# Two attentions in a written order, rope by halves, PSUM pools kept: many small edits to a two-block fp32 kernel

## The chip, the cores and the metric

One core of one Trainium2 chip. The metric is the time on the device of one execution in microseconds, median over the runs. TensorE is called PE below, its weight loads PEld, VectorE DVE, ScalarE ACT, GpSimd POOL, and SyncE, which issues nearly all DMAs, SP.

## What is computed

Two blocks on a sequence of 512 tokens of width 1024, all in float32. Block one puts 16 meta tokens ahead (528 columns) and adds to h in turn a SwiGLU layer, a mixer of two attentions, and a second SwiGLU layer, each behind a norm and followed by one:

```python
h = h + 0.5 * rmsnorm(swiglu(rmsnorm(h, g1), wg, wu, wd), post1)
p = rmsnorm(h, g) @ w_in            # sb_q sb_k sb_v c_q c_kv k_r gates
y_sb  = stick_breaking_attention(sb_q, sb_k, sb_v) @ w_sb_o    # 8 heads
q = rmsnorm(c_q) @ w_uq             # 64 plain + 32 turned dims per head
y_mla = latent_attention(q_nope, rope(q_rope), k_nope, rope(k_r), v) @ w_mla_o
h = h + rmsnorm((sigmoid(g_sb) * y_sb + sigmoid(g_mla) * y_mla) @ w_out, post2)
h = h + 0.5 * rmsnorm(swiglu(rmsnorm(h, g3), ...), post3)
```

Rope turns each pair (x1, x2) of half vectors to (x1 cos - x2 sin, x1 sin + x2 cos). Block two has two layers: a recurrence with an mLSTM (called hy), then attention in a window (swa), each followed by a convolved feed-forward layer (convffn) and a gated addition (ple).

## The kernel before, in words

Activations lie transposed, features on partitions and tokens on columns. Each float32 product is three passes of a rounded type: `whi` and `wlo` are a weight tile's high and low parts (ACT casts, DVE subtracts the cast, in `wload`, L286 and L287), `xh` and `xl` those of the activations. A linear with 8 k-tiles and 512 columns is 24 matmuls of 128x512 (L301 in `mm`, L328 in `lin_first`, which starts a phase with several outputs together). Raw weights (`wraw`) come by DMA in SP's order.

PSUM has pools named by `psums`: l (linears) and a (everything small) in most phases, z, l and a with two banks each in the two attentions. Each phase opens its own pools, and `rstd` sums the squares over partitions by a product with ones (L393), after DVE has added the eight squared tiles into `acc` (L247).

The scheduler orders all engines but, in the attentions, PE follows a hand-written order: for each pair of heads c and block b of 128 queries, `start` issues the scores (L721) and masks (L724), `chain` the softmax on ACT and DVE, `attn_t` transposes the probabilities `e` (L672, L684), and `attn_v` multiplies by the values (L695). Between them `fill(n)` puts n steps of the linears in `todo` (L343, `step_lin`): the next pair's projections, the gates, the output products. `step_lin` with `two=True` fills two banks (256 and 272 columns) in turns for `sbk` and the latent keys. In `attn_t` and `attn_v` all instructions stand in a block of raised priority, those of PE too.

In `latent`, two of the four pairs share a rope product: `uq` tiles 4 to 7 are the rope columns and the same columns with halves swapped, `t12` holds the two products with cos and sin, and DVE adds them into rows 64 to 95 of each q (96 rows). ACT copies q, k and the common `kr` rows into new tiles for each pair. `values` (L910) is computed between the first projection and the first scores. All 16 gate sigmoids stand before `latent`. In `hy`, `heads` ends with four transposes of `nm` back (L1120), directly behind the norm's scaling on DVE (L1119).

Of the kernel before, what the change touches and what calls it, by code (L numbers as in the profile page):

```python
# [72 lines left out]
def prep(inp):  # L73
# [18 lines left out]
    r["uq"] = np.concatenate([_wt(nope), _wt(rope), _wt(_swap(rope, 16))], axis=0)  # L92
# [72 lines left out]
def consts():  # L165
# [23 lines left out]
    r["rope"] = np.ascontiguousarray(rope.astype(np.float32))  # L189
# [26 lines left out]
class Kern:  # L216
    def __init__(self, tc, d, voff):
        self.tc, self.nc, self.d, self.voff = tc, tc.nc, d, voff
        self.act_cur, self.act_pre, self.act_epoch = None, None, []

# [33 lines left out]
    def psums(self, st, **bufs):  # L254
        self.psp = {n: st.enter_context(self.tc.tile_pool(name="ps" + n, bufs=b, space=PSUM, reuse_waits="tile"))
                    for n, b in bufs.items()}
# [23 lines left out]
    def wload(self, src, n, ahead=100):  # L280
        nc = self.nc
        raw = self.early.pop(0) if self.early else self.wdma(src, n)
        hi = self.wp.tile([P, 1024], F32R, name="whi", bufs=WB[1])[:, :n]
        lo = self.wp.tile([P, 1024], F32R, name="wlo", bufs=WB[1])[:, :n]
        with self.tc.high_priority(offset=ahead):
            nc.scalar.copy(hi, raw)  # L286
            nc.vector.tensor_tensor(lo, raw, hi, op=ALU.subtract)  # L287
# [48 lines left out]
    def step_lin(self, src, x, kc, done, c0=0, two=False):  # L336

        hi, lo = self.wload(src, kc * P, 2000)
        segs, ev = self.banks2() if two else self.banks1(c0)
        for k in range(kc):  # L340
            for pi, (a, b) in enumerate(((hi, x[0]), (hi, x[1]), (lo, x[0]))):
                for ps, t0, t1 in segs:
                    self.nc.tensor.matmul(ps, a[:, k * P:(k + 1) * P], b[:, k, t0:t1],  # L343
                                          start=k == 0 and pi == 0, stop=k == kc - 1 and pi == 2)
                yield
        with self.tc.high_priority(offset=1000):
            done(ev)
# [38 lines left out]
    def rstd(self, acc, tt, tb, dim, pool_r, name="r"):  # L386
# [5 lines left out]
        for i, (c, w) in enumerate(blocks):  # L392
            nc.tensor.matmul(ps[:w, i * 64:(i + 1) * 64], acc[:, c:c + w], self.ones[:, :64], start=True, stop=True)  # L393
# [52 lines left out]
    def square(self, acc, m, parts):  # L446
# [4 lines left out]
        for p, a, b in parts:  # L451
            self.act(sq[:, a:b], p, AF.Square)
        if m:
# [18 lines left out]
    def begin(self, st):  # L472
# [14 lines left out]
        nc.sync.dma_start(self.vecs, d["vecs"])  # L487
# [3 lines left out]
    def begin2(self):  # L491
        self.nc.sync.dma_start(self.cst, self.d["cst"])
# [3 lines left out]
    def ffn(self, n, h, tt, name):  # L496
# [5 lines left out]
        self.psums(n.st, l=6, a=2)  # L502
# [51 lines left out]
    def mixer(self, n, h):  # L554
        nc, d, tc = self.nc, self.d, self.tc
        mul, add = ALU.mult, ALU.add
        stP = ExitStack()
        self.psums(stP, l=6, a=2)
# [11 lines left out]
        with ExitStack() as stS:  # L570
# [3 lines left out]
            with ExitStack() as st:  # L574
                A = self.pool(st, "mA")
                rope = A.tile([64, 2, TM], F32, name="rope64")
                nc.sync.dma_start(rope, d["rope"][:64])
# [47 lines left out]
            stP.close()  # L625
            stP = ExitStack()
# [881 lines left out]
```

## Time and profile before

| what | value |
|---|---|
| median of 3 runs | 2532.71 us (2532.6 to 2533.84) |
| the profiled execution | 2533.2 us |
| its span, first to last instruction | 2531.4 us |
| PE busy | 2496.9 us (99%) |
| DVE, ACT, POOL busy | 54%, 39%, 6% |
| granted PE clock, mean | 1.0 |

The profile is of one core. A matmul's record runs from its start to a modelled end, and the next one may start before that. "Idle <- releaser" is the time in which the engine had no instruction, and what it waited for.

### The profile page before, as it was taken

The numbers are of one execution on the slowest core, as the hardware profiler recorded it, in microseconds if no ns is written. First come the engines' busy times: TensorE is split into PE (matmuls) and PEld (weight loads), VectorE is DVE, ScalarE is ACT, GpSimd is POOL, SyncE is SP. The second block draws the span as 40 slices with busy tenths as digits, with TensorE's granted clock in tenths as the row PEclk, the third lists the DMA queues.
The fourth block names the chain that finished last, engine by engine and source line by source line (L and its number), as shares of the span: only waits on it lengthen the run. The fifth ranks groups of instructions, "written<-read, shape, count | busy, mean of one in ns | idle before, by whom it ended". The sixth has DMA issues, their size and how long they took to land.

```text
span 2531.4 us, 33257 instructions
## 1 busy us (share of the span) xinstructions
PE 2496.9 (99%) x13334; PEld 2081.7 (82%) x13334; DVE 1360.7 (54%) x2197; ACT 993.6 (39%) x1601; POOL 162.3 (6%) x159
## 2 busy tenths in 40 slices
PE   8999999999999999999999999999999999999999
PEld 8999998777677788888777888888888668888887
DVE  5323347455566562434668765345465775535544
ACT  4222235344654442223564633223344563323332
POOL 1101010000001010101001011001000001101100
PEclk9999999999999999999999999999999999999999
DMA  4322234212212433333322332332333123333332
GB/s 140 92 92 85 92 95 132 81 54 67 59 43 64 161 116 92 97 100 98 115 89 90 118 107 91 93 109 92 93 114 101 42 76 133 94 98 100 96 89 100
DMA packets 78932, 240.49 MB, mean 95 GB/s; under 512 B 9332, under 2 KB 11636, under 8 KB 78520
## 3 DMA queue, kind: packets, MB, share of 16 engines
q1 hardware_dynamic: 78776, 238.35, 30.4%
q8 instruction: 105, 1.72, 0.3%
q14 instruction: 51, 0.42, 0.1%
HBM read 226.24 MB, written 8.92 MB: 93 GB/s over the span
## 4 chain that ended last, share of the span: by engine, by line
PE 91%; DVE 4%; ACT 3%; issue 1%; DMA 1%; POOL 0%; SPq 0%; ACTq 0%; DVEq 0%
PE l L301 71%; PE l L328 5%; PE l L343 5%; PE l L314 2%; PE z L721 1%; PE a L695 1%; PE a L672 1%; ACT e L236 1%; PE s L1414 1%; DVE wlo L287 1%; ACT whi L286 1%; PE a L408 1%; PE a L393 1%; DMA wraw<-in_hyo 1%; PE a L1442 1%
## 5 line engine op out<-in xcount | busy, mean ns | idle before, releaser
L286 ACT CAST whi<-wraw 128x1024 fp32r<-128x1024 f32 (+4 forms) x456 | 432.9, 950 | 1032.1 <-PE l L301 781.7
L301 PE MATMUL l<-xh,whi 128*128 128x512 f32 (+3 forms) x2156 | 707.9, 355 | 0.0
L301 PE MATMUL l<-xh,wlo 128*128 128x512 f32 (+3 forms) x2156 | 705.8, 354 | 0.0
L301 PE MATMUL l<-xl,whi 128*128 128x512 f32 (+3 forms) x2156 | 705.5, 354 | 0.0
L287 DVE TENSOR_TENSOR wlo<-wraw,whi 128x1024 fp32r<-128x1024 f32 (+4 forms) x456 | 500.2, 1098 | 274.9 <-ACT whi L286 268.8
L301 PEld LDWEIGHTS l<-xh,whi 128*128 128x128 f32 (+1 forms) x2156 | 382.1, 188 | 56.9 <-issue 1.4
L301 PEld LDWEIGHTS l<-xh,wlo 128*128 128x128 f32 (+1 forms) x2156 | 381.9, 188 | 56.6 <-issue 1.0
L301 PEld LDWEIGHTS l<-xl,whi 128*128 128x128 f32 (+1 forms) x2156 | 382.2, 187 | 56.2 <-issue 1.2
L301 PE MATMUL l<-chh,wlo 128*128 128x512 f32 x384 | 149.4, 389 | 0.0
L301 PE MATMUL l<-chl,whi 128*128 128x512 f32 x384 | 149.4, 389 | 0.0
L301 PE MATMUL l<-chh,whi 128*128 128x512 f32 x384 | 149.4, 389 | 0.0
L301 PE MATMUL l<-hh,wlo 128*128 128x256 f32 (+2 forms) x528 | 140.3, 320 | 0.0
L301 PE MATMUL l<-hl,whi 128*128 128x256 f32 (+2 forms) x528 | 140.2, 320 | 0.0
L301 PE MATMUL l<-hh,whi 128*128 128x256 f32 (+2 forms) x528 | 140.1, 319 | 0.0
L247 POOL TENSOR_TENSOR t<-g,xrs 128x528 f32<-128x528 f32 (+1 forms) x44 | 75.1, 1708 | 646.0 <-ACT g L236 646.0
L247 POOL TENSOR_TENSOR cc<-cc,xrs 128x512 f32<-128x512 f32 x48 | 62.8, 1308 | 834.1 <-ACT cc L236 830.3
L247 DVE TENSOR_TENSOR t<-l,t 128x256 f32<-128x256 f32 (+1 forms) x66 | 32.3, 516 | 143.9 <-PE l L301 138.9
L301 PEld LDWEIGHTS l<-hh,whi 128*128 128x128 f32 x528 | 88.4, 188 | 6.9
L301 PEld LDWEIGHTS l<-hl,whi 128*128 128x128 f32 x528 | 88.2, 188 | 6.9
L301 PEld LDWEIGHTS l<-hh,wlo 128*128 128x128 f32 x528 | 88.3, 188 | 6.8
L247 DVE TENSOR_TENSOR g<-l,xrs 128x256 f32<-128x256 f32 (+1 forms) x66 | 32.3, 516 | 114.3 <-PE l L301 112.6
L247 DVE TENSOR_TENSOR cz<-l,xrs 128x512 f32<-128x512 f32 x48 | 33.2, 692 | 109.6 <-PE l L301 105.3
(350 smaller groups left out, 3463.6 us busy)
## 6 DMA issues: line engine op xcount, KB each, us to landing
wraw<-in_up SPq DMA_DIRECT2D x96, 512.0 KB, 3.5
wraw<-in_dn SPq DMA_DIRECT2D x64, 384.0 KB, 3.2
wraw<-in_ffn_g SPq DMA_DIRECT2D x44, 512.0 KB, 3.5
wraw<-in_ffn_u SPq DMA_DIRECT2D x44, 512.0 KB, 3.4
wraw<-in_ffn_d SPq DMA_DIRECT2D x32, 448.0 KB, 3.3
wraw<-in_hy SPq DMA_DIRECT2D x20, 512.0 KB, 3.5
wraw<-in_ffn_d SPq DMA_DIRECT2D x16, 512.0 KB, 3.6
wraw<-in_gate SPq DMA_DIRECT2D x16, 512.0 KB, 3.5
```

What stands on the lines that cost most here:

```text
L236: i = nc.scalar.activation(out, in_, f, **kw)
L247: return (eng or self.nc.vector).tensor_tensor(out, a, b, op=op)
L286: nc.scalar.copy(hi, raw)
L287: nc.vector.tensor_tensor(lo, raw, hi, op=ALU.subtract)
L301: self.nc.tensor.matmul(ps, a[:, k * m:(k + 1) * m], b[:, k0 + k, c0:c1], start=first and k == 0 and pi == 0, stop=last and k == kc - 1 an ...
L314: self.nc.tensor.matmul(ps[:c1 - c0, :n], a[:, k, c0:c1], b[:, j * n:(j + 1) * n], start=k == 0 and pi == 0, stop=k == nk - 1 and pi == 2)
L328: self.nc.tensor.matmul(ps, a[:, k * P:(k + 1) * P], b[:, k0 + k, t0:t1], start=k == 0 and pi == 0, stop=k == kc - 1 and pi == 2)
L343: self.nc.tensor.matmul(ps, a[:, k * P:(k + 1) * P], b[:, k, t0:t1], start=k == 0 and pi == 0, stop=k == kc - 1 and pi == 2)
L393: nc.tensor.matmul(ps[:w, i * 64:(i + 1) * 64], acc[:, c:c + w], self.ones[:, :64], start=True, stop=True)
L408: nc.tensor.matmul(p[:, c - a:c - a + w], r[:w, i:i + 1].to_broadcast([w, P]), self.ident[:w, :w], start=True, stop=True)
L672: nc.tensor.transpose(pt[:, j * P:(j + 1) * P], probs[hh][:, i * P:(i + 1) * P], self.ident)
L695: nc.tensor.matmul(po[64 * hh:64 * hh + 64, :], vt[:, i, (2 * c + hh) * 64:(2 * c + hh + 1) * 64], where[(i, hh)], start=i == 0, stop=i == nb)
```

## The change

1. **Begin.** The first 8 columns of `vecs` and the first tile of h are loaded ahead of all weights; the first two weight tiles are loaded and cast in pieces of 256 and 768 columns.
2. **PSUM.** `psums` keeps the pools if the next phase asks for the same; the last phase of swa asks for l=6, a=2 like its neighbours.
3. **`step_lin` with two=True** computes the first half (256 columns) over all k, hands it on, then the second.
4. **Attentions.** In `attn_t` and `attn_v` only the copies keep the raised priority; PE's instructions stand in the order in which they are written.
5. **Latent.** The rope columns of all 8 heads are ordered by halves (two tiles, 18 matmuls in place of 36); six DVE instructions give `turned` once, DMAs of 32 rows put it into q (now 128 rows), k are four standing tiles whose `kr` rows are put there by DMA. The first projection's copies go to DVE, `values` behind the first scores; each pair has two `wo` products to fill with (before 2, 1, 2, 3). Only `gs` sigmoids stand ahead; those of `gm` go into the `wo` loop.
6. **w_out** splits its first weights at priority 2000.
7. **Squares.** The last of the eight squares isn't added by DVE: PE sums it in `rstd` with a second set of small matmuls, in the same bank (after ffn1, mixer and ffn2).
8. **hy.** The transposes back become `back`, called behind a further linear.

The core of the diff:

```diff
+    def psums(self, **bufs):
+        if bufs == self.ps_bufs:
+            return
+        self.ps_st.close()
...
-    def lin_first(self, srcs, x, kc, c0=0, wide=False, two=False, k0=0):
-        ws = [self.wload(src, kc * P) for src in srcs]
+    def lin_first(self, srcs, x, kc, c0=0, wide=False, two=False, k0=0, ahead=100):
+        ws = [self.wload(src, kc * P, ahead) for src in srcs]
...
     def step_lin(self, src, x, kc, done, c0=0, two=False):
-        segs, ev = self.banks2() if two else self.banks1(c0)
-        for k in range(kc):
+        for c0, c1 in ((0, CUT), (CUT, TM)) if two else ((c0, c0 + T),):
+            ps = self.bank()[:, :c1 - c0]
+            for k in range(kc):
...
+            with self.tc.high_priority(offset=1000):
+                done(ps, c0, c1)
...
+        accs = acc if isinstance(acc, list) else [acc]
+        for j, a in enumerate(accs):
+            for i, (c, w) in enumerate(blocks):
+                nc.tensor.matmul(ps[:w, i * 64:(i + 1) * 64], a[:, c:c + w], self.ones[:, :64],
...
+        if m == KD - 1:
+            return [acc, sq]
...
-        with self.tc.high_priority(offset=100):
-            for g0 in range(0, len(slots), 4):
+        for g0 in range(0, len(slots), 4):
...
+            with self.tc.high_priority(offset=100):
                 (nc.vector.tensor_copy if (g0 // 4) % 2 else nc.scalar.copy)(at[:, :n1], pt[:, :n1])
...
+                for s_ in range(2):
+                    p = 64 + 32 * s_ + 16 * hh
+                    nc.sync.dma_start(k[p:p + 16, :], kr[16 * s_:16 * s_ + 16, :])
...
+                        self.tt(turned[:, j, :], ps, rope[:, 0, :], mul)
+                        self.tt(t[:, 1 - j, :], ps, rope[:, 1, :], mul)
+                        if j:
+                            self.tt(turned[:, 0, :], turned[:, 0, :], t[:, 0, :], ALU.subtract)
+                            self.tt(turned[:, 1, :], turned[:, 1, :], t[:, 1, :], add)
...
-            nm = (2, 1, 2, 3)[c]
+            nm = 2
...
-            self.fill(6)
+            if c == 0:
+                values()
+            else:
+                self.fill(4)
...
-        first = self.lin_first([d["wout"][m] for m in range(2)], oo, KD)
+        first = self.lin_first([d["wout"][m] for m in range(2)], oo, KD, ahead=2000)
...
-            heads(hd, segs[hd])
+            nm = heads(hd, segs[hd])
+            if hd < 2:
+                z_of(5 + 2 * hd, bias=False, out=gg[:, 2 * hd + 1, :])
...
+            back(hd, nm)
-        kn.early.append(kn.wdma(d[("ffn1_g", "ffn1_u")[k]][0], D))
+        for a, b in ((0, 2 * P), (2 * P, D)):
+            for w, nm in zip(kn.early, ("ffn1_g", "ffn1_u")):
+                dma(w[:, a:b], d[nm][0][:, a:b])
```

Three places where the order of instructions moves. **PE, stick-breaking attention, first pair of heads, block 0 to 1.** z are scores, a<-cst,e the transposes of the probabilities, idb the mask's product, l<-x a linear step. Before:

```order
L343 MATMUL l_5010<-xl_4215,whi_5006 128x512
L721 MATMUL z_5051<-sbk_4911,sbq_4910 128x272 x2
L672 MATMUL a_5103<-cst_62,e_5024 128x128 x2
L684 MATMUL a_5103<-cst_62,e_5024 16x128 x2
L724 LDWEIGHTS idb_65
L724 MATMUL z_5051<-masks_4362,idb_65 128x128
```

Now:

```order
L354 MATMUL l_5085<-xl_4227,whi_5081 128x256
L690 MATMUL a_5106<-cst_62,e_5028 128x128 x2
L703 MATMUL a_5106<-cst_62,e_5028 16x128 x2
L354 MATMUL l_5085<-xh_4226,wlo_5082 128x256
L354 MATMUL l_5085<-xh_4226,whi_5081 128x256
```

The transposes stood right behind block 1's scores and ahead of their masks; now the masks come first and 24 linear matmuls stand between the scores and the transposes.

**PE, the same stage, the keys' projection `sbk`.** l_5081 and l_5082 are its two banks before, l_5085 and l_5119 now. Before:

```order
L343 MATMUL l_5081<-xh_4214,whi_5077 128x256
L343 MATMUL l_5082<-xh_4214,whi_5077 128x272
L343 MATMUL l_5081<-xl_4215,whi_5077 128x256
L343 MATMUL l_5082<-xl_4215,whi_5077 128x272
L343 MATMUL l_5081<-xh_4214,wlo_5078 128x256
L343 MATMUL l_5082<-xh_4214,wlo_5078 128x272
```

Now:

```order
L354 MATMUL l_5085<-xl_4227,whi_5081 128x256
L354 MATMUL l_5085<-xh_4226,wlo_5082 128x256
L354 MATMUL l_5119<-xh_4226,whi_5081 128x272
L354 MATMUL l_5119<-xl_4227,whi_5081 128x272
L354 MATMUL l_5119<-xh_4226,wlo_5082 128x272
```

Both banks ended together; now the first is complete 24 matmuls before the second.

**SP, from the stick-breaking to the latent attention.** wraw are weight tiles, rope the tables. Before:

```order
L277 DMA wraw_6635<-in_uk 128x256 [waits DMAHW3_49,DVE_49]
L830 DMA rope_6570<-in_rope 128x1056 [waits DVE_49,PE_49,Pool_49]
L277 DMA wraw_6663<-in_uv 128x1024 [waits DMAHW4_49,DVE_49]
L277 DMA wraw_6724<-in_uq 128x384 [waits DMAHW5_49,DVE_49]
L277 DMA wraw_6760<-in_uk 128x256 [waits DMAHW7_49,DVE_49]
```

Now (behind rope8 and seven DMAs of kr):

```order
L863 DMA k11_6568<-kr_4362 16x528 [waits DMAHW1_49,Pool_49]
L890 DMA q0_6637<-turned_6581 32x512 [waits DMAHW2_49,DVE_49]
L890 DMA q0_6637<-turned_6581 32x512 [waits DMAHW3_49]
L890 DMA q1_6641<-turned_6581 32x512 [waits DMAHW4_49]
L890 DMA q1_6641<-turned_6581 32x512 [waits DMAHW5_49]
L890 DMA q0_6804<-turned_6581 32x512 [waits DMAHW6_49]
L890 DMA q0_6804<-turned_6581 32x512 [waits DMAHW7_49]
L890 DMA q1_6808<-turned_6581 32x512 [waits DMAHW0_49]
L890 DMA q1_6808<-turned_6581 32x512 [waits DMAHW1_49]
L863 DMA k11_6568<-kr_4362 16x528 [waits DMAHW2_49]
L285 DMA wraw_6753<-in_uq 128x384 [waits DMAHW3_49,Activation_49]
L285 DMA wraw_6812<-in_uk 128x256 [waits DMAHW4_49,DVE_49]
```

The weights of the second pair stood behind the tables alone; now they stand behind eight DMAs that wait for `turned`.

## Rows read from the trace of the kernel before

**Rows 1.** The page's part 1, busy time of each engine over the span.

```profile
PE 2496.9 (99%) x13334; PEld 2081.7 (82%) x13334; DVE 1360.7 (54%) x2197; ACT 993.6 (39%) x1601; POOL 162.3 (6%) x159
```

**Rows 2.** Stages: window, length, busy PE, PEld, DVE, ACT, POOL, granted clock, DMA share, GB/s.

```profile
684.00:694.00 10.00, 7.63 (x39) 6.25 (x38) 6.62 (x10) 9.83 (x19) 0.00 (x0) 1.00 0.42 115
694.00:795.00 101.00, 98.63 (x657) 72.58 (x656) 63.78 (x178) 54.90 (x145) 0.00 (x0) 1.00 0.14 43
```

**Rows 3.** Timeline of the beginning: start us, us, engine, line, operation, [idle before <-releaser].

```profile
1.65 0.43 SPq L1463 DMA_DIRECT2D h<-in_xT  x1
...
7.32 0.73 ACT L244 ACTIVATE xh<-h,vecs 128x528 fp32r<-128x528 f32 x1 [1.56 <-DMA h<-in_xT]
...
8.11 0.58 PE L328 MATMUL l<-xh,whi 128*128 128x256 f32 x1 [8.11 <-ACT xh L244]
```

**Rows 4.** DMA issues over the span: KB each, us from issue to landing.

```profile
qt<-ra SPq DMA_DIRECT2D x32, 64.0 KB, 2.0
...
rope<-in_rope SPq DMA_DIRECT2D x1, 528.0 KB, 3.7
...
vecs<-in_vecs SPq DMA_DIRECT2D x1, 213.5 KB, 2.6
```

**Rows 5.** Timeline of PE where hy and its feed-forward layer begin.

```profile
1233.31 0.47 PE L301 MATMUL l<-pph,whi 128*128 128x512 f32 x1 [0.88 <-ACT whi L286]
...
1461.74 0.47 PE L328 MATMUL l<-xh,whi 128*128 128x512 f32 x1 [1.63 <-DVE h L247]
```

**Rows 6.** Groups of instructions on PE, whole span: busy, mean ns | idle before <-releaser.

```profile
L343 PE MATMUL l<-xh,whi 128*128 128x512 f32 (+2 forms) x224 | 79.2, 370 | 2.1 <-DVE sbk L247 2.1
L672 PE MATMUL a<-cst,e 128*128 128x128 f32 x160 | 27.1, 282 | 5.1 <-ACT e L236 3.9 <-DVE e L894 1.1
```

**Rows 7.** Timeline of PE at a rope product of the latent stage.

```profile
683.12 0.39 PE L343 MATMUL l<-cqh,whi 128*128 128x512 f32 x1
683.35 0.39 PE L343 MATMUL l<-cql,whi 128*128 128x512 f32 x1
```

**Rows 8.** Timeline from the last stick-breaking product to the end of the latent stage.

```profile
678.02 0.44 PE L695 MATMUL a<-rest,sbv 128*64 128x128 f32 x4
678.54 0.33 SPq L830 DMA_DIRECT2D rope<-in_rope  x1
684.65 0.69 DVE L247 TENSOR_TENSOR t<-l,rope 128x512 f32<-128x512 f32 x1
691.13 0.40 PE L343 MATMUL l<-ckvh,whi 128*128 128x272 f32 x1 [2.37 <-ACT q L243]
...
736.63 0.39 PE L343 MATMUL l<-ckvh,whi 128*128 128x272 f32 x1 [0.73 <-ACT q L243]
...
791.13 0.44 PE L672 MATMUL a<-cst,e 128*128 128x128 f32 x2 [1.09 <-DVE e L894]
```

**Rows 9.** Stages, the columns of rows 2: the first matmuls of the program.

```profile
8.10:13.40 5.30, 5.28 (x19) 4.47 (x20) 4.12 (x6) 4.93 (x8) 0.00 (x0) 1.00 1.01 385
```

**Rows 10.** Timeline at the first products of w_out.

```profile
816.54 1.22 DVE L287 TENSOR_TENSOR wlo<-wraw,whi 128x1024 fp32r<-128x1024 f32 x1
...
817.82 0.50 PE L328 MATMUL l<-ooh,wlo 128*128 128x512 f32 x1 [1.50 <-DVE wlo L287]
```

**Rows 11.** Timeline of PE at the sums of squares after ffn1 and the mixer.

```profile
404.41 1.12 PE L393 MATMUL a<-cst,acc 128*88 128x64 f32 x12 [0.81 <-DVE acc L247]
...
864.48 1.08 PE L393 MATMUL a<-cst,acc 128*128 128x64 f32 x8 [1.96 <-DVE acc L247]
865.37 0.48 PE L301 MATMUL l<-ppl,whi 128*128 128x512 f32 x1
```

**Rows 12.** Timeline of PE at the norm's way back in hy, heads 0, 1 and 3.

```profile
1391.26 0.44 PE L1120 MATMUL a<-cst,nm 128*128 128x128 f32 x2 [0.35 <-DVE nm L1119]
...
1407.76 0.83 PE L1120 MATMUL a<-cst,nm 128*128 128x128 f32 x4 [0.26 <-DVE nm L1119]
...
1429.95 0.30 PE L1120 MATMUL a<-cst,nm 128*128 128x128 f32 x1 [0.43 <-DVE nm L1119]
```

More of the change, by code (lines that the diff above doesn't have):

```diff
@@ L638, in mixer @@
             if True:
-                self.latent(st, cq, ckv, kr, masks[:, P:], ymla, ysb, gs)
-        stP.close()
-        self.psums(n.st, l=6, a=2)
+                self.latent(st, cq, ckv, kr, masks[:, P:], ymla, ysb, gs, lambda: [sigmoid(gs, m) for m in range(KD)])
+        self.psums(l=6, a=2)
         O = self.pool(n.st, "O")
@@ L644, in mixer @@
         fs = O.tile([P, KD, T], F32, name="mfs")
+        for m in range(2):
+            sigmoid(gm, m)
         for m in range(KD):
+            if m < KD - 2:
+                sigmoid(gm, m + 2)
             ps = self.lin1(d["wo"][m][:, 512:], ymla, 4)
@@ L834, in latent @@
         nc.gpsimd.memset(vt[:, 4, :], 0.0)
-        t12 = L.tile([P, 2, T], F32, name="t12")
+        ks = [[L.tile([P, TM], F32, name=f"k{hh}{i}") for i in range(2)] for hh in range(2)]
+        for i in range(2):
+            for hh in range(2):
+                k = ks[hh][i]
+                nc.gpsimd.memset(k[64:, :], 0.0)
+                for s_ in range(2):
+                    p = 64 + 32 * s_ + 16 * hh
+                    nc.sync.dma_start(k[p:p + 16, :], kr[16 * s_:16 * s_ + 16, :])
+        turned = L.tile([P, 2, T], F32, name="turned")
@@ L903, in latent, with values @@
         self.fill()
[L904 to L912 removed]
+        def values():
+            w = self.wload(d["uv"][0], 1024)
+            for i in range(5):
+                a, b = i * P, min((i + 1) * P, TM)
+                ps = self.bank()[:b - a]
+                for k in range(2):
+                    for pi, (xx, ww) in enumerate(((0, 0), (1, 0), (0, 1))):
+                        nc.tensor.matmul(ps, ckv[xx][:, k, a:b], w[ww][:, k * 512:(k + 1) * 512],
+                                         start=k == 0 and pi == 0, stop=k == 1 and pi == 2)
+                self.copy(vt[:b - a, i, :], ps)
+        sigmoids()
         late, m = None, 0
         for c in range(4):
[L915 removed]
+            nm = 2
             self.todo = ([proj(c + 1)] if c < 3 else []) + [wo(m + i) for i in range(nm)]
@@ L1151, in hy @@
             if hd > 1:
-                for m in range(4 * hd - 8, 4 * hd - 4):
+                out(4 * hd - 8)
+            back(hd, nm)
+            if hd > 1:
+                for m in range(4 * hd - 7, 4 * hd - 4):
                     out(m)
```

190 lines of the change are left out of this document (92 added, 98 removed).

## The prediction

> **What bounds the kernel now.** I read the page's busy shares first: PE is busy 99% of a 2531.4 us span, no other engine much above half [rows 1]. So only two things shorten the kernel: PE work that goes away, and the 2531.4 - 2496.9 = 34.5 us in which PE stands idle. Then I read the stages, to see where that idle time lies: 2.4 us of 10 and 2.4 of 101 in the two windows of the latent stage [rows 2], the rest in short pieces elsewhere. Last I read, wait by wait, what released PE [rows 3, 5, 6, 8, 10 to 12]. The reader should see there that no wait but the first is over 2.4 us, and that they come from five kinds of cause: a PSUM bank not yet drained, a softmax not finished, a weight split late, a sum of squares, the first load.
>
> How real is an idle figure? Two linear matmuls start 683.35 - 683.12 = 0.23 us apart, but each record lasts 0.39 [rows 7]. A wait is counted from the modelled end, so up to 0.16 us of each is booked as busy. The Trainium skill (Perfetto Trace Analysis, Identifying the Most-Contended Engine) says TensorE's busy share is a poor measure, since pipelined instructions overlap in the trace; by that rule some 20 removed waits (counted one by one in the timeline) would each give up to 0.16 us more, 3.2 us in all. The records' overlap agrees. I keep the idle figures in the sum and put the extra into a rival, because a stream that is interrupted by another kind of matmul drains anyway.
>
> **The change part by part**, in us; minus is faster.
>
> *Begin: -2.6.* The first tile of h is issued at 1.65 behind weights and reaches ACT only at 7.32; PE starts at 8.11 [rows 3]. A load of 213.5 KB at the queue's head landed in 2.6 [rows 4]. The tile, now ahead of the weights, should land at about 1.65 + 2.6 = 4.3 plus a little for its 264 KB, the rounding takes 0.73, and the cut weights queue behind it: first matmul at 5.5. Bounds -1.0 (the 19 matmuls that take 5.30 us there [rows 9] are held by later loads) and -3.3.
>
> *PSUM kept: -2.5.* hy's first matmul waits 0.88 and convffn's 1.63 [rows 5], both the first in pools just opened, while the last output of the phase before is being added to h or fs. Now both phases take the next of six banks. The row names ACT whi for the first; if that is the true cause, 0.9 stays. Bounds -0.7, -2.5.
>
> *sbk by halves: -2.1.* The keys' projection waits 2.1 for DVE to drain two banks that end together [rows 6]. Now the first half is drained under the 24 matmuls of the second. Bounds -1.0, -2.6.
>
> *Attentions in written order: -3.5 + 1.7.* Transposes wait 3.9 for the exponentials of ACT [rows 6]; with 24 linear matmuls (24 x 0.23 = 5.5 us) between them and the scores, little of that is left; I take -3.5, between bounds of -3.9 and 0. What is late next is the chain at the end of a pair, below. Against it, the linears are cut into more runs: 44 to 48 in the stick-breaking stage, 45 to 52 in the latent one. The first linear after a small matmul lasts 0.48 instead of 0.39 [rows 7, 11]: 0.09 on entering, and I allow as much on leaving, with bounds of nothing and 0.3: 11 runs x 0.15 = +1.7.
>
> *Rope once: -4.1.* 18 matmuls of 0.23 [rows 7] fewer, and PE has nothing else to do instead. This is the surest term. DVE loses eight additions of q rows and gains four others; it is half idle. The eight ACT copies of kr, and with them the wait of 0.73 for ACT q at 736.63 [rows 8]: -0.7.
>
> *Stick-breaking to latent: +0.6.* The tables' load is issued when the last value product has ended: 678.54 against 678.02 + 0.44 [rows 8]. So the new, equally large tables land 3.7 later [rows 4], at 682.2. Six DVE instructions of 0.69 [rows 8] give `turned` at 686.4; SP issues the four q DMAs in steps of 0.33 and a DMA of 64 KB takes 2.0 [rows 4], so q0 is there at 688.7, q1 at 689.4. PE has 42 linear matmuls from 678.5, 30 whole ones and 12 halves: 30 x 0.23 + 12 x 0.12 = 8.3, until 686.8. It waits about 2 for q0, then has values to compute; with two l banks drained by the same DVE I add 1. That is 3 where 2.37 stood. Bounds -2.4 and +2.5. The second pair's weights now stand behind eight q DMAs on SP: 686.4 + 8 x 0.33 = 689.0, landed by some 2.6 later, while 27 value matmuls (6.2 us) cover PE until about 695; nothing.
>
> *Latent tail: +1.5.* The last pair has two `wo` products to fill with, not three: 12 x 0.23 = 2.8 us less cover, where 1.09 of waiting for the softmax stands already [rows 8]. Bounds 0, +4.
>
> *w_out: -1.5.* PE waits 1.50 because DVE splits the first weights late, from 816.54 [rows 10]. The higher priority brings the split ahead of the mixing work, for which PE doesn't wait there. Bounds -1.5, 0.
>
> *Squares: +0.3.* 14 more small products. Four cost 865.37 - 864.48 = 0.89 [rows 11], so 14 at most 3.1; the six after ffn1 are narrower, and I take 2.7, and 0.3 for three more interruptions. They give back 0.7 of the first wait (one DVE addition, as long as the row of DVE in [rows 8]) and the 1.96 of the second, under which the sums of seven and five linears now run: -2.7. After ffn2 there was no wait to give back. Bounds -0.8, +1.5.
>
> *hy's way back: -0.9.* Of three waits 0.35 and 0.26 go behind a linear; the 0.43 of head 3 stays, since its place is the same [rows 12]; two interruptions fewer. Bounds -1.3, 0.
>
> The sixteen sigmoids that move on ACT hide in its idle half; one table load more is uncovered only if `wo` waits for it.
>
> Sum: -2.6 - 2.5 - 2.1 - 3.5 + 1.7 - 4.1 - 0.7 + 0.6 + 1.5 - 1.5 + 0.3 - 0.9 = -13.8. The profiled execution took 2533.2, the median is 2532.7, half a microsecond less; so 2533.2 - 13.8 = 2519.4, as a median **2518.9**. All low ends together give -23, all high ends +5; they don't come together.
>
> **Rivals.**
>
> *Waits that move.* The waits for the exponentials, for w_out, in hy and at sbk come back as others, on DVE, which drains what is now ready sooner: the 8.0 of these terms are lost, 2526.9. For: in the latent stage DVE is busy 64 of 101 us and ACT 55 [rows 2], each step of a chain is behind the one before. Against: the order shows 24 matmuls where none stood. Chance 0.20.
>
> *More is covered.* Interruptions cost nothing, the transition and the tail are hidden, and the overlapped 0.16 us come back for some waits: -13.8 - 1.7 - 0.6 - 1.5 = -17.6, or 2515.1, down to 2512. Chance 0.20.
>
> *SP blocks the latent stage (slower).* The q DMAs of the later pairs wait for PE and stand on SP's one queue ahead of weights. If each holds the weights behind it until the pair before has been scored, a pair's linears (9 of uq, 12 halves of uk, 24 of wo: 33 x 0.23 + 12 x 0.12 = 9 us) run behind its attention instead of under it. Three pairs cost 27 us: 2546. It decides from two pairs on, since 13.8 + 5.1 must be eaten. Against: q has two buffers, and the reader waited for is two pairs back. Chance 0.05.
>
> *The clock falls in the transition.* In this trace the granted clock reads 1.00 (2.4 GHz) in the ten us that hold the wait of 2.37 and in the whole latent stage [rows 2]. Yet after 8.11 us without work the 19 half matmuls took 5.30 us [rows 9], 3.0 more than at 0.12 each; a wait of 3 that did the same would give 2521.9. The Trainium skill (TensorE: Matmul & The Clock Gate, Part 1) says an idle array drops to 1.2 GHz and must be busy a while to get back; no row of a short wait here shows it. Chance 0.03.
>
> That the change doesn't do what it says is excluded by the order for PE and SP; only whether the moved instructions find their data ready is open.
>
> **How the numbers follow.** The forecast has the remaining 0.52, spread over about 2511 to 2526. The measurement can't tell less than 0.2%, 5.1 us, from no change: the edges are 2527.6 and 2537.8. Faster: 0.52 + 0.20 + 0.03 + 0.12 of the moving waits = 0.87. Within 0.2%: 0.08 of these and 0.01 of the blocked queue, 0.09. Slower: 0.04. The range, **2509 to 2529**, leaves out about 0.18: the worse half of the first rival, the third, and what lies below.
>
> **What would show it.** Right: the first PE instruction near 5.5; no idle before the first matmul of hy and convffn; no releaser DVE sbk, and ACT e under 1 us; the latent stage shorter by 3 to 5; a single wait of 2 to 4 us before the first latent scores, released by a q DMA. Wrong: ACT e or DVE e of several us in the latent stage (rival 1), SP issues of wraw more than 10 us apart between 700 and 790 with PE idle (rival 3), PE busy the same though the 18 matmuls are gone.

## Result and the profile after

The changed kernel takes **2504.15 us** (median of 4 runs, 2503.73 to 2504.66); the kernel before took 2533.28 beside it. The ratio is 0.9884, interval 0.9867 to 0.9902: 29.1 us faster. The forecast was 2518.9, with a range of 2509 to 2529: the sign was right, the gain was twice what was forecast, and the time lies below the range.

Page of the changed kernel, part 1, and the first line of part 4 (the chain that ended last, shares by engine):

```profile
PE 2482.8 (99%) x13344; PEld 2082.0 (83%) x13344; DVE 1357.7 (54%) x2194; ACT 986.2 (39%) x1588; POOL 163.4 (7%) x163
...
PE 96%; ACT 2%; DVE 1%; issue 1%; DMA 0%; SPq 0%; POOL 0%; ACTq 0%; DVEq 0%
```

The span is 2502.4, 29.0 less. Against [rows 1], PE has ten matmuls more in the records and is busy 14.1 us less; its idle time falls from 34.5 to 2502.4 - 2482.8 = 19.6, by 14.9. So only half of the gain is idle time that went away, the quantity on which most of the prediction's sum was built. The 18 rope products that went are 4.1 of the busy half (18 x 0.23). The rest of it is the question of this study.

Where the gain lies was read from the starts of the same PE instructions in both traces:

| stretch | before | after | difference |
|---|---|---|---|
| start to first matmul | 8.11 | 5.21 | -2.9; at the last matmul of ffn1 -1.9 |
| first to last PE instruction of the stick-breaking stage | 182.9 | 170.4 | -12.5 |
| from there to the first product of the latent attention's output (`ymh`) | 111.0 | 105.1 | -5.9 |
| w_out | 45.6 | 43.6 | -2.0 |
| all up to hy's first linear | 1241.22 | 1214.83 | -26.39 |
| all up to the first feed-forward product behind hy | 1461.74 | 1432.78 | -28.96, constant from there on |

The stick-breaking stage of the changed kernel also holds some eleven gate products (2.5 us) that stood behind it before, so that stage gained about 15 and the latent one about 3.4. The two stages, before and then after: window, length, busy PE, PEld, DVE, ACT, POOL, granted clock, DMA share, GB/s.

```profile
495.30:678.20 182.90, 177.07 (x1027) 130.32 (x1026) 106.73 (x172) 84.58 (x153) 3.39 (x31) 1.00 0.18 56
678.20:789.20 111.00, 107.35 (x683) 80.24 (x682) 68.48 (x183) 66.82 (x167) 0.00 (x0) 1.00 0.17 51
```

```profile
492.10:662.50 170.40, 169.85 (x1039) 131.59 (x1040) 105.54 (x175) 88.54 (x159) 2.99 (x30) 1.00 0.20 61
662.50:767.60 105.10, 99.52 (x654) 74.37 (x651) 67.28 (x183) 50.09 (x138) 2.53 (x5) 1.00 0.22 65
```

In the stick-breaking stage PE was idle 5.8 us and is idle 0.6, 5.2 less; yet twelve matmuls more take 7.2 us less of busy time. Idle time can't explain the stage.

The waits of PE as groups of the changed kernel (line, engine, operation, tiles, count, busy, mean ns, idle before it and releaser):

```profile
L354 PE MATMUL l<-xh,whi 128*128 128x512 f32 (+2 forms) x224 | 83.2, 371 | 0.1
L690 PE MATMUL a<-cst,e 128*128 128x128 f32 x160 | 23.8, 273 | 1.2 <-DVE e L927 1.2
L354 PE MATMUL l<-cqh,whi 128*128 128x512 f32 x18 | 7.5, 419 | 2.6 <-DVE t L250 2.6
L1163 PE MATMUL a<-cst,nm 128*128 128x128 f32 x16 | 3.3, 294 | 0.6 <-DVE nm L1157 0.6
```

The first two answer to [rows 6]: the linears' wait, for DVE sbk before, fell from 2.1 to 0.1, and the transposes' wait for ACT e from 3.9 to nothing. The timeline of the changed kernel at the other places of [rows 3, 5, 8, 10 to 12]:

```profile
5.21 0.58 PE L338 MATMUL l<-xh,whi 128*128 128x256 f32 x1 [5.21 <-ACT whi L296]
...
408.42 0.40 PE L338 MATMUL l<-xh,whi 128*128 128x512 f32 x1
...
669.74 0.47 PE L354 MATMUL l<-cqh,whi 128*128 128x512 f32 x1 [2.63 <-DVE t L250]
...
673.60 0.36 PE L354 MATMUL l<-ckvh,whi 128*128 128x272 f32 x1 [0.87 <-DVE q L888]
...
792.90 0.39 PE L338 MATMUL l<-ooh,whi 128*128 128x512 f32 x1
...
836.71 1.00 PE L408 MATMUL a<-cst,acc 128*128 128x64 f32 x8
...
1206.50 1.00 PE L408 MATMUL a<-cst,acc 128*128 128x64 f32 x8
1207.31 0.48 PE L311 MATMUL l<-pph,whi 128*128 128x512 f32 x1
...
1402.77 0.30 PE L1163 MATMUL a<-cst,nm 128*128 128x128 f32 x1 [0.43 <-DVE nm L1157]
...
1432.78 0.39 PE L338 MATMUL l<-xh,whi 128*128 128x512 f32 x1
```

The reader should see which brackets are gone: none stands where hy (1207.31) and convffn (1432.78) begin, none at w_out (792.90), none at the sums of squares (836.71 after the mixer, 1206.50 after ffn2). The wait between the two attentions is there as foreseen, 2.63 and 0.87, and the last head's 0.43 in hy stayed.

### The profile page after: what moved, and what is told of

The parts are those of the page before. It is cut to its first block, busy times and chain, and to the rows that moved or that the text cites. A ratio compares the mean times of both kernels' runs of the same rounds, so it can differ in the third digit from the quotient of the medians.

```text
span 2502.4 us, 33319 instructions
## 1 busy us (share of the span) xinstructions
PE 2482.8 (99%) x13344; PEld 2082.0 (83%) x13344; DVE 1357.7 (54%) x2194; ACT 986.2 (39%) x1588; POOL 163.4 (7%) x163
## 4 chain that ended last, share of the span: by engine, by line
PE 96%; ACT 2%; DVE 1%; issue 1%; DMA 0%; SPq 0%; POOL 0%; ACTq 0%; DVEq 0%
PE l L311 73%; PE l L354 6%; PE l L338 6%; PE l L324 2%; PE z L741 1%; PE a L714 1%; PE s L1459 1%; PE a L408 1%; PE a L424 1%; PE a L690 1%; PE a L1487 1%; PE a L1481 0%; ACT e L239 0%; PE l L1129 0%; DVE wlo L297 0%
```

## Experiments

Each is timed beside the kernel before on the same chip. That kernel's own median lay between 2532.53 and 2533.54 there, and the last column subtracts medians that were not taken side by side, so a difference of under about 1 us in it tells nothing by itself.

| run | median us | ratio to before, interval | against the changed kernel |
|---|---|---|---|
| scores not side by side | 2513.23 | 0.9923 (0.9908 to 0.9938) | +9.1 |
| written order alone | 2518.13 | 0.9941 (0.9927 to 0.9956) | +14.0 |
| raised priority again | 2526.66 | 0.9972 (0.9962 to 0.9983) | +22.5 |
| latent of before | 2508.79 | 0.9904 (0.9887 to 0.9921) | +4.6 |
| squares added by DVE | 2511.03 | 0.9916 (0.9901 to 0.9931) | +6.9 |
| squares alone | 2527.97 | 0.9982 (0.9972 to 0.9992) | +23.8 |
| PSUM reopened | 2506.78 | 0.9899 (0.9882 to 0.9915) | +2.6 |
| begin of before | 2505.82 | 0.9893 (0.9876 to 0.9909) | +1.7 |
| key halves in turns | 2505.40 | 0.9892 (0.9877 to 0.9907) | +1.3 |
| hy's way back at once | 2504.24 | 0.9889 (0.9874 to 0.9904) | +0.1 |
| early rope table | 2500.97 | 0.9876 (0.9861 to 0.9891) | -3.2 |
| early table, copies on ACT | 2499.80 | 0.9866 (0.9849 to 0.9882) | -4.4 |

### What the written order brings

The trace gave the first theory, A. The scores z of two heads are products over 64 rows each, head 0 on rows 0 to 63 of the array, head 1 on rows 64 to 127. Where the two follow each other directly, their records run at the same time. In the kernel before, PE instructions of raised priority go between the two heads' scores of the longer blocks (400 and 264 columns) and pull them apart. Against it stood the prediction's own account: removed waits, and cheap or dear interruptions. First PE's timeline of the kernel before at two blocks' scores, then the same scores of the changed kernel:

```profile
518.75 0.71 PE L721 MATMUL z<-sbk,sbq 64*128 64x264 f32 x2
519.39 0.66 PE L672 MATMUL a<-cst,e 128*128 128x128 f32 x4
519.88 0.38 PE L684 MATMUL a<-cst,e 128*16 128x128 f32 x2
520.19 0.71 PE L721 MATMUL z<-sbk,sbq 64*128 64x264 f32 x2
520.83 0.66 PE L695 MATMUL a<-at,sbv 128*64 128x128 f32 x8
521.42 0.72 PE L721 MATMUL z<-sbk,sbq 64*128 64x264 f32 x4
522.06 0.44 PE L695 MATMUL a<-at,sbv 128*64 128x128 f32 x4
```

```profile
512.91 1.16 PE L741 MATMUL z<-sbk,sbq 64*128 64x264 f32 x8
```

The trace shows each score product as two matmuls. The two of one head alone hold PE until 0.64 later (518.75 to 519.39, 520.19 to 520.83). Four of two heads as neighbours hold it no longer (521.42 to 522.06), and eight last 1.16 by their records.

**Scores not side by side.** The changed kernel, with head 0's queries in a tile of 128 rows whose rows 64 to 127 are zeros, so that its product takes the whole array:

```diff
-                nc.vector.scalar_tensor_tensor(q, ps, 0.125, rs[:, META:], op0=mul, op1=mul)
+                nc.vector.scalar_tensor_tensor(q0[c % 2][:64], ps[:64], 0.125, rs[:64, META:], op0=mul, op1=mul)
+                nc.vector.scalar_tensor_tensor(q[64:], ps[64:], 0.125, rs[64:, META:], op0=mul, op1=mul)
...
+            qh = lambda hh: q[64:] if hh else q0[c % 2]
+            self.scores(units, lambda hh: qh(hh)[:, b * P:(b + 1) * P], lambda hh: k[64:] if hh else k, mask)
```

> The changed kernel, but in the stick-breaking attention head 0 of each pair scores over all 128 rows, with zeros in the other head's 64 rows, instead of over its own 64; the order on PE stays, no linear is moved. Theory A (two score products of 64 rows each, one on the upper and one on the lower half of the array, run side by side when they are neighbours; the change made them neighbours): they run one after the other again, 8 products each of 144 columns at 0.43 us, 8 of 272 and 16 of 264 at 0.64, 8 of 400 at 0.87 = 25.8 us in place of 13.4, so about 12 us slower than the changed kernel, near 2516. Theory B (what the forecast missed in this stage are waits for the exponentials that were longer than their idle time): the waits stay away, so within 1 us of the changed kernel's 2504.

Measured: 9.1 us slower than the changed kernel, and its stick-breaking stage is 180.2 long, not 170.4. The same eight score matmuls in its timeline:

```profile
512.79 0.60 PE L741 MATMUL z<-sbk,sq 128*128 128x264 f32 x2
513.33 0.71 PE L741 MATMUL z<-sbk,sbq 64*128 64x264 f32 x2
513.97 0.71 PE L741 MATMUL z<-sbk,sq 128*128 128x264 f32 x2
514.61 0.71 PE L741 MATMUL z<-sbk,sbq 64*128 64x264 f32 x2
```

They take 514.61 + 0.71 - 512.79 = 2.53 instead of 1.16, and the full rows are no dearer than the half ones (0.54 and 0.64 to the next start). The order of PE and its waits are nearly those of the changed kernel; only the neighbours are lost. That is theory A. But the 9.1 are not yet the share of the gain: this run takes apart all pairs of heads, and in the kernel before some still stood side by side. The table below has the share.

**Written order alone.** The kernel before with part 4, and nothing else:

```diff
-        with self.tc.high_priority(offset=100):
-            for g0 in range(0, len(slots), 4):
+        for g0 in range(0, len(slots), 4):
...
+            with self.tc.high_priority(offset=100):
                 (nc.vector.tensor_copy if (g0 // 4) % 2 else nc.scalar.copy)(at[:, :n1], pt[:, :n1])
```

> The kernel before with the written order alone (raised priority for the copies only in attn_t and attn_v, in both attentions). Theory A: scores become neighbours (-9) and the waits for the exponentials go (-4 to -6), a few more interruptions: about -13, near 2520. The prediction's own step (-3.5 + 1.7): near 2531. Theory C (the gain comes only with the keys' halves and the shorter latent stage): near 2533.

Measured: 2532.82 - 2518.13 = 14.7 us faster than the kernel before, half of the whole change. Its groups:

```profile
L343 PE MATMUL l<-xh,whi 128*128 128x512 f32 (+2 forms) x224 | 80.3, 373 | 0.7 <-DVE sbk L247 0.5
...
L671 PE MATMUL a<-cst,e 128*128 128x128 f32 x160 | 24.1, 272 | 0.3 <-DVE yml L247 0.3
L722 PE MATMUL z<-sbk,sbq 64*128 64x264 f32 x32 | 4.7, 409 | 0.0
```

Against [rows 6] the transposes' waits fell from 5.1 to 0.3, and the linears' from 2.1 to 0.7 although the keys' halves still end together. The whole account of the two attentions, from the first score to the first product of w_out, comes from the four profiles: for each matmul the time from its start to the next one's, without the idle time between them.

| us | before | order alone | changed | not side by side |
|---|---|---|---|---|
| PE idle | 10.7 | 4.4 | 6.9 | 6.7 |
| stick-breaking scores | 20.7 | 13.3 | 13.7 | 24.6 |
| transposes of e | 24.4 | 21.9 | 21.6 | 21.6 |
| value products | 31.0 | 30.0 | 30.1 | 30.1 |
| linears (934, 934, 916, 916) | 211.7 | 212.2 | 205.8 | 204.5 |
| latent scores, all masks | 21.6 | 22.1 | 22.8 | 22.9 |
| sum | 320.2 | 303.8 | 300.8 | 310.4 |

The order alone brings 7.4 in the scores, 6.4 of idle time, and 3.5 in transposes and value products, which now stand in longer runs. The linears take 0.4 more, where the prediction put +1.7 for more interruptions. In the changed kernel the scores' share is 7.0; the run with zeros adds 10.9 to them, and its linears take 1.2 less.

Not all of the 7.0 is overlap. A lone pair of matmuls of 264 columns takes 0.33 and 0.31 to the next start. In the run of eight at 512.91 the four pairs of neighbours take 0.33, 0.22, 0.22 and 0.31, so a run of scores has a slow beginning and a slow end, and three short runs pay for them three times.

At the first product of w_out the profile of this run is 18.4 ahead of the kernel before, at its end 14.2. It loses the rest where the granted clock reads 0.50 (1.2 GHz, against 2.4): from 799.5 to 802.8 and from 847.3 to 854.0, behind waits of PE of 1.51 and 1.97. The profile of the kernel before has these waits too, and its clock reads 1.00.

**Raised priority again.** The changed kernel with part 4 undone:

```diff
-        for g0 in range(0, len(slots), 4):
+        with self.tc.high_priority(offset=100):
+            for g0 in range(0, len(slots), 4):
```

> The changed kernel with the transposes and value products of both attentions at raised priority again (part 4 undone), all else as changed. Alone, part 4 brought 14.7 us. If the parts add up: near 2518 to 2519, score products apart again and waits for ACT e of some us. If keys by halves and the new fills had kept the scores together anyway: below 2510. The prediction's step (-3.5 + 1.7) says 2506.

Measured: 22.5 us slower than the changed kernel, 7.8 more than part 4 brought alone. Its groups:

```profile
L691 PE MATMUL a<-cst,e 128*128 128x128 f32 x160 | 29.2, 291 | 7.2 <-ACT e L239 6.6 <-DVE e L926 0.4
L740 PE MATMUL z<-k,q 128*128 128x264 f32 (+3 forms) x80 | 26.9, 439 | 3.5 <-ACT e L239 2.4 <-DMA q<-turned 1.1
```

The latent stage is 120.0 long instead of 105.1. PE comes to a pair's transposes, and then to the scores behind them, while ACT is still at the exponentials; the new `latent` leans on the written order. Parts 4 and 5 are not additive. But the waits are not all: in three stretches, 13.6 us together, the granted clock is 0.50. The first of them (columns as in the stages above):

```profile
683.10:689.80 6.70, 5.96 (x17) 3.39 (x17) 3.30 (x11) 2.21 (x9) 0.00 (x0) 0.50 0.52 152
```

At half the clock the three can cost up to 6.8 of the 22.5 us. The other two (693.3 to 696.6 and 788.9 to 792.2) begin right behind waits for ACT e of 1.93 and 3.39.

### The latent stage

**Latent of before.** The changed kernel with the old `latent`: two rope products, `t12`, `kr` copied by ACT, all sigmoids ahead.

```diff
-                    yield from self.step_lin(d["uq"][4 + j], cq, 3, turn(j))
+                    yield from self.step_lin(d["uq"][4 + 2 * j + c // 2], cq, 3, turn(j))
...
-                    for s_ in range(2):
-                        nc.sync.dma_start(q[64 + 32 * s_:96 + 32 * s_, :], turned[32 * c:32 * c + 32, s_, :])
+                    self.tt(q[64:96], t12[32 * i:32 * i + 32, 0, :], t12[32 * i:32 * i + 32, 1, :], add)
```

> The changed kernel with the latent stage's projections, rope, fills and values of the kernel before (in the written order of the change; the gs sigmoids stand ahead of it). If part 5 is worth what the prediction's terms say (18 matmuls -4.1, a wait -0.7, transition +0.6, tail +1.5, runs +1.0), it is 1.7 us slower than the changed kernel, near 2506. If the matmuls count in full and transition and tail are no loss, near 2509 to 2510.

Measured: 4.6 us slower, where the prediction's terms make 4.1 + 0.7 - 0.6 - 1.5 = 2.7, and 1.7 with the 7 x 0.15 of its runs. Not all of the 4.6 is the latent stage. In w_out a wait of 0.88 for DVE wlo is back, though part 6 is in place, and that stage is 1.4 longer. Behind the wait of 2.86 between the attentions, linears start 0.43 apart instead of 0.23, and the granted clock from 669.4 to 672.7 reads 0.50.

**Early rope table.** The two tables (cos and sin) go into tiles of the square sums' pool and are loaded before the stick-breaking attention, not behind its last value product.

```diff
+            self.rope8 = [self.st.tile([P, TM], F32, name="sq", bufs=2)[:, :T] for _ in range(2)]
+            for i in range(2):
+                nc.sync.dma_start(self.rope8[i], d["rope8"][:, i, :])
...
-        rope = L.tile([P, 2, T], F32, name="rope")
-        nc.sync.dma_start(rope, d["rope8"])
+        rope = self.rope8
```

> The changed kernel with the two rope tables loaded before the stick-breaking attention, into two tiles that stand idle there, instead of behind its last product. If the table is what the 2.6 us wait between the attentions hangs on: near 2501.5. Rival (the chain of six DVE instructions, the copies and the q DMAs ends last anyway): 2503 to 2504, the wait only moved to the first scores.

The chain that this cuts, in the timeline of the changed kernel:

```profile
663.19 0.38 SPq L849 DMA_DIRECT2D rope<-in_rope  x1
...
668.31 0.69 DVE L250 TENSOR_TENSOR turned<-l,rope 128x512 f32<-128x512 f32 x1 [2.57 <-DMA rope<-in_rope]
...
672.02 4.94 SPq L890 DMA_DIRECT2D q<-turned  x8
```

DVE idles 2.57 for the table, and PE then 2.63 for DVE. Measured: 3.2 us faster than the changed kernel. Some of that may be the clock's: all eight executions of this run and the next read a mean granted clock of 1.000, two of the four of the changed kernel 0.999. The one wait left on PE there (timeline of this run):

```profile
670.39 0.36 PE L354 MATMUL l<-ckvh,whi 128*128 128x272 f32 x1 [1.19 <-DVE q L890]
```

**Early table, copies on ACT.** The same, and the first pair's copies of q and k back on ACT:

```diff
-            copy = nc.vector.tensor_copy if c == 0 else self.copy
+            copy = self.copy
```

> The early rope tables, and the first projection's copies of q and k on ACT (idle there for 6.3 us in that run's trace) instead of DVE. If the 1.2 us wait for DVE q is what stands there: near 2500, 1.0 to 1.3 under the run with the early tables alone. If the DMAs into q end last: unchanged.

```profile
669.14 0.39 PE L354 MATMUL l<-ckvh,whi 128*128 128x272 f32 x1 [0.56 <-ACT q L246]
```

Measured: 2499.80, the fastest of all, 1.2 under the run before it. The wait fell by 1.19 - 0.56 = 0.63; the rest is within what two such medians differ by. With DVE no longer held up by the table, there is no reason to keep these copies on it.

### The squares

**Squares added by DVE.** The changed kernel without part 7:

```diff
-        if m == KD - 1:
-            return [acc, sq]
```

> The changed kernel with the last of the eight squares added by DVE again (part 7 undone). Forecast: part 7 is worth nothing (+0.3), so 2504. Rival, from the stages of the two traces (ffn1 to mixer 1.3 less, mixer to ffn2 1.1 less): near 2506.5, with the waits for DVE acc back.

Measured: 6.9 us slower, where the prediction had part 7 at +0.3. In the trace the loss isn't at the sums: waits for ACT xh stand before the first matmul of the *next* norm's linear, 1.55, 1.97 and 1.53 us (5.0 in all), and 1.7 more for its `xl`. The timeline of this run, and then the kernel before at the same place:

```profile
406.03 0.39 PE L311 MATMUL l<-pph,wlo 128*128 128x512 f32 x1
406.23 1.04 ACT L296 CAST whi<-wraw 128x1024 fp32r<-128x1024 f32 x1 [0.52 <-PE l L311]
407.18 1.36 ACT L247 ACTIVATE xh<-h,vecs 128x528 fp32r<-128x528 f32 x2
407.96 0.50 PE L338 MATMUL l<-xh,whi 128*128 128x512 f32 x1 [1.55 <-ACT xh L247]
```

```profile
409.72 1.36 ACT L244 ACTIVATE xh<-h,vecs 128x528 fp32r<-128x528 f32 x2
410.98 1.04 ACT L286 CAST whi<-wraw 128x1024 fp32r<-128x1024 f32 x1
```

The products that fill PE between the sum and the next norm (`pph`) have run out, and a weight cast that waits for the last of them stands ahead of `xh` on ACT. In the kernel before, `xh` came first. That the cast is 1.04 long and ahead is shown; why the scheduler puts it there without part 7 wasn't tried.

The waits are not the whole loss. Behind the first two of them, and behind the one between the attentions, the granted clock is 0.50 for some 3 us each; the first:

```profile
409.10:412.40 3.30, 3.14 (x7) 2.48 (x8) 3.30 (x8) 2.16 (x4) 0.00 (x0) 0.50 0.69 236
```

How much of the 6.9 is the clock's was not separated.

**Squares alone.** The kernel before with part 7, and nothing else:

```diff
+        accs = acc if isinstance(acc, list) else [acc]
+        for j, a in enumerate(accs):
...
+        if m == KD - 1:
+            return [acc, sq]
```

> The kernel before with part 7 alone (the last square summed by PE). If part 7 is worth by itself what undoing it cost (6.8): near 2526. Forecast (+0.3): 2533. If its worth depends on what the other parts did to the order of the next norm's work: between, with the wait for DVE acc of 1.96 after the mixer gone and another in its place.

Measured: 2532.87 - 2527.97 = 4.9 us faster than the kernel before, interval 2.0 to 7.1. The two profiles differ by 2.4 at the three places (1.15, 0.5, 0.75), and by more in the start and the first layer, ahead of the first of these places. hy's first wait of 0.88 ([rows 5]) goes with part 7: there is none at that place here. So part 7 alone is worth between 2.4 (its places) and 4.9 (the medians); in the changed kernel, where the cast comes first without it, undoing it cost 6.9. The clock may have a share in the medians too: five of these nine executions read 1.000, of the twelve of the kernel before beside them one.

### Small parts

**PSUM reopened.** `psums` opens new pools each time:

```diff
-        if bufs == self.ps_bufs:
-            return
```

> The changed kernel, but every phase opens PSUM pools of its own again (part 2 undone). Forecast: 0.9 in hy and 1.6 in the first convffn come back, 2.5, near 2506.7. The stages of the two traces say 1.3 and 2.0: 2507.5. Rival (the phases that follow attentions or ffn1 hide it): below 2505.

```profile
1435.12 0.47 PE L336 MATMUL l<-xh,whi 128*128 128x512 f32 x1 [1.30 <-DVE h L250]
```

Measured: +2.6. The wait for h is back where convffn begins and is 1.30 of it. At hy's first matmul no wait is seen, so the 0.88 there was not the pools'. Besides, by the traces w_out and the sum behind it are 1.2 longer (waits of 0.17 for DVE ool and 0.57 for ACT sq), and so is the way from the last stick-breaking product to the first latent score, with the granted clock at 0.50 from 668.1 to 671.4. That the pools have a part in these isn't shown.

**Begin of before.** The loads at the start as they were:

```diff
-        nc.sync.dma_start(self.vecs[:, :KD], d["vecs"][:, :KD])
+        nc.sync.dma_start(self.vecs, d["vecs"])
...
-        dma(h[:, 0, :], d["xT"][0])
```

> The changed kernel with the loads of the beginning in the order of the kernel before, whole first weights (part 1 undone). Forecast 2.6: near 2506.7. The first matmul's start in the two traces (8.1 against 5.2) says at most 2.9; the end of the first feed-forward layer says 1.9: 2506.

Measured: +1.7. But its trace doesn't show the loss in the first layer. PE starts at 6.69, 1.5 later than in the changed kernel, yet the last matmul of ffn1 starts at 398.30, between the 397.92 and 399.35 of the runs with part 1; the run with the order alone, without part 1, has 399.29. What is longer lies behind: 1.3 between the attentions, with the granted clock at 0.50 from 668.3 to 671.6, and 1.0 in w_out (waits of 0.48 and 0.23 for ooh and ool). So a gain by part 1 is not shown beyond the first matmuls.

**Key halves in turns.** Part 3 undone in `step_lin`:

```diff
-        for c0, c1 in ((0, CUT), (CUT, TM)) if two else ((c0, c0 + T),):
-            ps = self.bank()[:, :c1 - c0]
-            for k in range(kc):
+        segs = self.banks2()[0] if two else [(self.bank()[:, :T], c0, c0 + T)]
+        for k in range(kc):
```

> The changed kernel with the two halves of the keys' projections computed in turns again (part 3 undone). Forecast: 2.1 us, with the drained overlap 2.6: near 2506.5, waits for DVE sbk back in the trace. Rival (the two banks are now drained under the linears of the written order anyway): 2504.

Measured: +1.3, about what two such medians can differ by. The waits for sbk are 0.5, not 2.1: the written order had already put the drain behind other work. The stick-breaking stage of its trace is 0.7 longer, and 1.0 is lost between the attentions, where matmuls start 0.43 apart:

```profile
669.65 0.47 PE L353 MATMUL l<-cqh,whi 128*128 128x512 f32 x1 [2.48 <-DVE t L250]
...
671.16 0.63 PE L353 MATMUL l<-cqh,wlo 128*128 128x512 f32 x1
671.58 0.63 PE L353 MATMUL l<-cqh,whi 128*128 128x512 f32 x1
```

The granted clock of that stretch:

```profile
670.60:673.90 3.30, 3.30 (x11) 2.70 (x11) 2.08 (x5) 0.00 (x0) 0.00 (x0) 0.50 0.13 33
```

**hy's way back at once.** Part 8 undone:

```diff
-            nm = heads(hd, segs[hd])
-            if hd < 2:
-                z_of(5 + 2 * hd, bias=False, out=gg[:, 2 * hd + 1, :])
+            heads(hd, segs[hd])
```

> The changed kernel with the four transposes back directly behind the norm's scaling in hy (part 8 undone). Forecast: 0.9, near 2505, waits for DVE nm of 1.0 in place of 0.6. Rival (the wait is only moved to the next reader): 2504.

Measured: +0.1. The waits for nm are 1.0 instead of 0.6, and even these 0.4 don't show in the time.

## Why the prediction was right in direction and wrong in size

| step of the prediction | forecast | what the runs show |
|---|---|---|
| attentions in written order | -3.5 + 1.7 | -14.7 alone |
| sbk by halves | -2.1 | -1.3 at most, 0.7 of it in its stage; the rest of the wait went with the written order |
| rope once, transition, tail, with their runs | -1.7 | -4.6, of which 1.4 in w_out |
| squares | +0.3 | up to -6.9 in the changed kernel, -2.4 to -4.9 alone |
| PSUM kept | -2.5 | -2.6, of which 1.3 at convffn and none at hy |
| begin | -2.6 | -1.7, not found in the first layer |
| w_out | -1.5 | wait of 1.50 gone, stage 2.0 shorter (no run of its own) |
| hy's way back | -0.9 | -0.1 |

**The step that failed is "Attentions in written order: -3.5 + 1.7".** It counted the idle waits that the new order covers, and sized them somewhat low: 3.5, where the transposes' waits fell by 4.8. It took PE's own work as fixed but for the price of interruptions, and put that at +1.7, where the linears took 0.4 more. But what a matmul costs PE depends on its neighbours: the scores gave 7.4 with the order alone, transposes and value products 3.5. The kernel before could have told it: at 521.42 in its timeline above four matmuls hold PE as long as two at 518.75. Its groups hint at it, and the prediction drew on none like them (groups of the stick-breaking window by form):

```profile
L721 PE MATMUL z<-sbk,sbq 64*128 64x264 f32 x32 | 9.9, 435 | 0.0
L721 PE MATMUL z<-sbk,sbq 64*128 64x400 f32 x16 | 7.4, 545 | 0.3
```

32 x 0.435 is 13.9, yet busy is 9.9. A busy time under count times mean says that records overlap: 0.71 of it here, and 7.4 of 16 x 0.545 = 8.7, or 0.85, in the other group. By itself the share doesn't tell why, since records of matmuls behind each other overlap too (the transposes of [rows 6]: 27.1 of 160 x 0.282 = 45.1, or 0.60). The same groups of the changed kernel:

```profile
L741 PE MATMUL z<-sbk,sbq 64*128 64x400 f32 x16 | 5.1, 541 | 0.0
L741 PE MATMUL z<-sbk,sbq 64*128 64x264 f32 x32 | 4.7, 409 | 0.0
```

The mean of one is nearly as before, 541 and 409 ns, but busy is 0.59 and 0.36 of count times mean. The groups' busy time has fallen by 2.3 and 5.2, 7.5 together.

The Trainium skill (TensorEngine Tiling (Array Packing), Key Properties) says that different tiles of the array can execute their matmuls in parallel. The trace agrees: the two heads' records start 7 ns apart when they are neighbours. The order rows ahead of the prediction show block 1, whose two heads were neighbours in the kernel before as well. For the longer blocks a reader who asks "which rows of the array does each use" could have priced it: 0.64 for the four matmuls of a pair of heads in place of 1.28.

**The second term that was off is "Squares: +0.3".** It priced PE's instructions, +2.7 and +0.3, and the waits at the sums, -2.7. It left out that this sum is on the path to the *next* norm, whose scale, `xh` and first linear come behind it. When the products that fill PE there run out, each of those us is lost. DVE's addition of 0.69 taken out of that path brought 1.15, 0.5 and 0.75 at the three places where part 7 stood alone; in the changed kernel without part 7 the cast also came ahead of `xh`, and two of the waits were followed by half the clock.

**The latent stage** is 3.4 shorter by the stages. The wait between the attentions came where the prediction put it (2.63 + 0.87, and 0.34 behind them, are 3.84, against a forecast of 3 and 2.37 before). The releaser was DVE, not a q DMA, since DVE itself waited for the table. At the tail 0.24, 0.37, 0.51 and 0.73 are 1.85, where 1.09 stood: +0.8, not +1.5. With these sizes the terms make 4.1 + 0.7 - 1.5 - 0.8 = 2.5 without any cost of seven more runs. Undoing part 5 cost 4.6: w_out is 1.4 of it, and its profile holds a stretch at half the clock. The +1.0 for the runs has no support in any run. The rival "More is covered" was right in that, and only in that; its 2515.1 is still 11 us too slow.

**Right were** the place of every wait that was to go, and that neither SP nor DVE takes over as the bound. PSUM was right in its total by luck, since hy's 0.9 was not the pools'. w_out was right in the changed kernel, but part 6 alone doesn't do it: with the old `latent` 0.88 of that wait stands, with the raised priority 1.42.

**The rival of the clock** did not occur in the profile of the changed kernel: the granted clock is 1.00 in both stages, the one with the wait of 2.63 included. But it does occur. In six runs that differ from the changed kernel by one part (latent of before, PSUM reopened, key halves, squares by DVE, hy's way back, begin of before) it reads 0.50 for some 3 us behind that wait of 2.1 to 2.9. In five of them the way from the last stick-breaking product to the first latent score is the same work as in the changed kernel: there it takes 14.0 to 14.6, and in the two profiles at 1.00 (changed kernel, scores not side by side) 12.9 and 13.4. So a fall costs about 1 us, not the 3.0 of that rival. Why it comes in one execution and not in another isn't shown. Differences of 1 to 2 us between these runs need not be those of the parts alone. The clock of 1.00 in [rows 9] isn't what the matmuls there show: those of 256 columns start 0.21 apart up to 13.5 and 0.12 from 13.9 on, as at half the clock and at the full one.

Of "Waits that move" little is seen in the latent stage (1.2 for DVE e, where 1.1 stood); in hy 0.6 of the waits for nm is left.

Undone one at a time, the parts give 1.7 + 2.6 + 1.3 + 22.5 + 4.6 + 6.9 + 0.1 = 39.7, without w_out. The whole is 29.1. The sum of terms was never exact for parts that share a wait or an order, and the clock enters some of them; the written order is the part on which others lean. A forecast that adds up single parts should say so in its range.

**What stays open:** why the cast and `xh` change places on ACT without part 7, the 2.5 us of "squares alone" that lie outside its three places, what part 1 brings, and how much of each small difference is the clock's.

## What to carry to other kernels

Before forecasting an order of matmuls, list the rows of the array that each uses: of two products over 64 rows on opposite halves the second is nearly free if they are neighbours, and a full-height product between them costs the pair its overlap. Compare the time to the next start where they are neighbours and where they aren't. Read the granted clock of each run behind the waits before giving a microsecond to a part. And price work that ends a phase (a sum, a norm) by the path to the next phase's first product, not by the instructions alone; then undo the parts one by one, since their gains don't add.

## What the runs showed of the hardware that was not expected

The two matmuls of 264 columns over 64 rows of each of two heads, four in all, hold PE some 0.64 us as neighbours, and 1.28 one head after the other. With zeros in the other 64 rows, a product over 128 rows is no dearer than one over 64: 0.54 to 0.64 to the next start, against 0.64. In the latent attention the queries grew from 96 to 128 rows, and the scores there take 19.2 us from start to start, against 18.6 before.

A linear behind a small matmul shows a longer record (0.48 instead of 0.39 us, [rows 7, 11]), yet cutting them into more runs cost 0.4 in all: where part 4 stood alone, the 934 linears of the two attentions take 212.2 from start to start, against 211.7.

Waits of PE of 1.5 to 3.4 us were followed, in some executions and not in others, by some 3 us or more at a granted clock of 0.50 (1.2 GHz), in which linears of 512 columns start 0.43 apart instead of 0.23.
